# An encoder layer with gathered and dense experts: v sums of one gathered tile moved behind the dense weights, and weight loads of 1 MB

## The chip, the cores and the metric

One NeuronCore of a Trainium2 chip runs the whole program in one launch. The metric is device time in microseconds (us); three timed runs of the kernel before gave 3608.81, 3620.37 and 3621.52, a median of 3620.37.

## What is computed

One layer of a streaming encoder, in float32, over two request groups that share one set of weights: a prompt of 1024 rows and a sample of 64 rows, 1024 columns each. The layer projects the normed rows (`w_in`, 9224 columns), mixes three branches (an mLSTM memory, a spatial gating unit, cross-attention into 256 memory rows), projects back (`w_out`), and adds PEER, an expert layer:

```python
q = (xb @ w_pq)                                  # 8 heads, two half keys each
v1, i1 = lax.top_k(s1, 16); v2, i2 = lax.top_k(s2, 16)
sc, pos = lax.top_k(cand, 16)                    # cand: all 16 x 16 sums of v1 and v2
e = cidx at pos; g = softmax(sc)                 # 128 experts of 16384 for each row
a = gelu(einsum('tkd,td->tk', u_exp[e], xb))
out = einsum('tk,tkd->td', g * a, v_exp[e])
```

A final RMSNorm follows. `u_exp` and `v_exp` have 16384 rows of 1024 floats, 64 MB each.

## The kernel before

The 1088 rows are nine tiles: 0 to 7 of the prompt (128 rows each) and "s" (64 rows). **Phase 1** runs them in three blocks, [0, 1], [2, 3, 4, "s"] and [5, 6, 7], through all projections. Every float32 product is three passes on TensorE: the weights are split in a high and a low part (`w_split`, L267: ScalarE makes `wh` at L277, VectorE subtracts for `wl` at L280) and each piece of 128 rows by 512 columns, here called a *split*, is one `wh` and one `wl`. Pieces come from DRAM by `w_load` (L253) on SP's queue: 512 KB each, two splits, three buffers `wraw` and in phase 2 a fourth, `wrawx`. A new load is issued when a piece's last split is made.

The expert layer is done in two ways. Tiles 2, 3, 4 and 5 are **dense**: all 16384 experts go through TensorE in **phase 2** (`hidden` L1108 for u, L1268 to L1270 for v), each hidden value multiplied by its weight. These weights (mostly zeros) are made before that by the loop at L1189 to L1222: VectorE makes one-hot rows (L1197, L1201), TensorE multiplies them (L1210), and they go to DRAM (`gd`) and come back (`g`, L1098). When the last are made, the signal "weights" is given.

Tiles 0, 1, "s", 6 and 7 (`GT`) are **gathered** (`experts`, L939). Each of 128 columns (64 for "s") of such a tile needs two operations: *u* gathers 128 rows of `u_exp` by an indirect DMA that GpSimd issues (L1025, 512 KB) and takes their dot products on VectorE (L1038); *v* gathers rows of `v_exp` and adds them, each times its weight `w`, into `gacc` (L1046; for the last tile into `gx`). A u and a v buffer set of 3 and 4 (`gu`, `gv`) bounds what is under way. There are 576 u and 576 v operations; their list `ops` (L989) pairs the u of one tile with the v of the tile before. The weights `w` of a tile (`w2`, L959) need all its u; the `ops` wait for "weights" at the last u of "s" (L1066 to L1068), and tiles 6 and 7 are chosen only after it (L847).

What stands where on each engine is fixed when the program is built: `Flow` (L29) runs the generators by the costs that they yield (2.5 or 2.2 for each gathered operation, L1071), and a scheduler orders what they record. On the chip each engine then works through its list in order, and waits at each semaphore.

The v sum that is moved, and the retrieval whose chosen experts it shares VectorE with (`top16`, L797), stand in this code:

Of the kernel before, what the change touches and what calls it, by code (L numbers as in the profile page):

```python
# [7 lines left out]
F32 = mybir.dt.float32  # L8
# [6 lines left out]
ALU = mybir.AluOpType  # L15
# [3 lines left out]
D = 1024  # L19
# [6 lines left out]
O_Q, O_K, O_V, O_IG, O_FG, O_OG, O_SU, O_SV, O_XQ, O_GT = 0, 512, 1024, 2048, 2052, 2056, 3080, 4104, 5128, 6152  # L26
# [39 lines left out]
def tile_stream_step(ctx: ExitStack, tc: tile.TileContext, a: dict, out: dict):  # L66
    nc = tc.nc
    V, S, T, G, SP = nc.vector, nc.scalar, nc.tensor, nc.gpsimd, nc.sync
# [21 lines left out]
    mp = first.enter_context(tc.tile_pool(name="mp", bufs=1))  # L90

    BU, BV = 3, 4
    RAW, HL = 3, 4

    now = {"dp": None}

# [47 lines left out]
        return t  # L144

    wg_raw = mp.tile([128, KD, 8], F32, name="wg_raw", tag="sA")
    G.dma_start(wg_raw, a["w_in"][:, O_IG:O_IG + 8].rearrange("(k p) c -> p k c", p=128))

    wgh = mp.tile([128, 2, KD, 4], F32R, name="wgh")
    wgl = mp.tile([128, 2, KD, 4], F32R, name="wgl")  # L150
# [91 lines left out]
    pieces = []  # L242

    def want(src, c0):
        for kp in range(4):
            pieces.append(src[kp * 256:(kp + 1) * 256, c0:c0 + 512].rearrange("(k p) c -> p k c", p=128))


    POOL = 192, 224
    W = {"load": 0, "split": 0, "got": 0}  # L250
    raw_t, split_t = {}, {}

    def w_load():  # L253
        i = W["load"]
        if i >= len(pieces):
            return
        src = pieces[i]

        if now["dp"] is None or i % (RAW + 1):
            t = wp.tile([128, D], F32, name="wraw", bufs=RAW)  # L260
        else:
            t = now["dp"].tile([128, D], F32, name="wrawx")
        SP.dma_start(t.rearrange("p (k c) -> p k c", k=src.shape[1]), src)
        raw_t[i] = t
        W["load"] += 1

    def w_split():  # L267
        i = W["split"]
        if i >= 2 * len(pieces):
            return  # L270
        p, kk = divmod(i, 2)
        while W["load"] <= p:
            w_load()
        t = raw_t[p][:, kk * 512:(kk + 1) * 512]
        h = wp.tile([128, 512], F32R, name="wh", bufs=HL)
        l = wp.tile([128, 512], F32R, name="wl", bufs=HL)
        S.copy(h, t)  # L277

        E = G if POOL[0] <= i < POOL[1] else V
        E.tensor_tensor(l, t, h.bitcast(F32), op=ALU.subtract)  # L280
        split_t[i] = (h, l)
        W["split"] += 1
        if kk == 1:
            raw_t.pop(p)
            w_load()

    def w_get():
        i = W["got"]
        while W["split"] <= min(i + HL - 1, 2 * len(pieces) - 1):
# [45 lines left out]
    st = {}  # L335
# [233 lines left out]
    def want_block():  # L569
        for c in (O_K, O_Q, O_V, O_V + 512, O_SV, O_SV + 512, O_SU, O_SU + 512, O_GT + D, O_GT + D + 512,  # L570
                  O_XQ, O_XQ + 512, O_OG, O_OG + 512, O_GT, O_GT + 512, O_GT + 2 * D, O_GT + 2 * D + 512):
            want(a["w_in"], c)
        for c in (0, 512):
            want(a["w_out"], c)
        for c in (0, 512, 1024, 1536):
            want(a["w_pq"], c)

    def main():
        mem = memory()
# [10 lines left out]

    for nm in ("w_mk", "w_mv"):
        for c in (0, 512):
            want(a[nm], c)
    for _ in BLOCKS:
        want_block()

# [3 lines left out]
    GP = 4  # L600
    LG = 4

    def want_u(m):
        if m < NP:
            for r in range(2):
                pieces.append(a["u_exp_t"][r * 512:(r + 1) * 512, m * 256:(m + 1) * 256]
                              .rearrange("(k p) e -> p k e", p=128))

    for m in range(LG):
        want_u(m)  # L610
    for g in range(NP // GP):
        for j in range(2 * GP):
            if j % 2 == 0:
                want_u(GP * g + j // 2 + LG)
            hf, q = divmod(j, GP)
            e0 = (GP * g + q) * 256
            pieces.append(a["v_exp"][e0:e0 + 256, hf * 512:(hf + 1) * 512].rearrange("(k p) c -> p k c", p=128))


    def mlstm():  # L620
# [174 lines left out]
    NC = 54  # L795

    def top16(v, i, src, n):  # L797
        w = kp.tile([128, 128], F32, name="tk", bufs=4)[0:src.shape[0]]
        V.max(v[:, 0:8], src)
        V.max_index(i[:, 0:8], v[:, 0:8], src)  # L800
        V.match_replace(w[:, 0:n], v[:, 0:8], src, NEG)
        V.max(v[:, 8:16], w[:, 0:n])
        V.max_index(i[:, 8:16], v[:, 8:16], w[:, 0:n])
# [36 lines left out]
    def choose_tile(b, t):  # L840

        L = ROWS_OF[t]
# [6 lines left out]
        pos = kp.tile([128, 8, 16], U32, name="pos", bufs=1)[0:L]  # L849
# [14 lines left out]
        q = kp.tile([128, 6, 128], BF, name="pq_")[0:L]  # L864
# [34 lines left out]
        if t not in DENSE:  # L899
# [3 lines left out]
            e = gp.tile([128, 128], I32, name="e", bufs=3)  # L903

            for q in range(128 // L):
                V.scalar_tensor_tensor(e[q * L:q * L + L, 0:L], ef[:, q * 64:q * 64 + L], 128.0,
                                       ef[:, 128 + q * 64:128 + q * 64 + L], op0=ALU.mult, op1=ALU.add)
        gg = kp.tile([128, 8, 16], F32, name="ggd")[0:L]
        V.tensor_tensor(gg, scv, scv[:, :, 0:1].to_broadcast([L, 8, 16]), op=ALU.subtract)
        S.activation(gg, gg, AF.Exp)  # L910
        sm = kp.tile([128, 8], F32, name="ksm")[0:L]
# [18 lines left out]
    GT = [t for t in TILES if t not in DENSE]  # L930
# [8 lines left out]
    def experts():  # L939

        st_u, st_v, st_x = {}, {}, {}
# [12 lines left out]
        def end_u(t):  # L954
            _, av = st_u.pop(t)
            e, gg = st.pop(("e", t))
            L = ROWS_OF[t]
            av, gg = av[:, 0:L], gg[:, 0:L]
            t1 = gp.tile([128, 128], F32, name="w2", bufs=2)[:, 0:L]  # L959
            if t == GT[2]:  # L960
                V.tensor_copy(t1[0:1, 0:1], st["weights"][0:1])
            S.activation(t1, av, AF.Square, scale=GELU_C ** 0.5)
            V.scalar_tensor_tensor(t1, t1, 1.0, av, op0=ALU.add, op1=ALU.mult)
            S.activation(t1, t1, AF.Tanh, scale=GELU_S)
            V.scalar_tensor_tensor(t1, t1, 1.0, av, op0=ALU.add, op1=ALU.mult)
# [24 lines left out]
        for k in range(len(GT) + 1):  # L990
            u = [("u", GT[k], j) for j in range(ROWS_OF[GT[k]])] if k < len(GT) else []
            v = [("v", GT[k - 1], j) for j in range(ROWS_OF[GT[k - 1]])] if k > 0 else []
            m = max(len(u), len(v))
            for j in range(m):
                for l in (u, v):
                    lo, hi = j * len(l) // m, (j + 1) * len(l) // m
                    ops += l[lo:hi]
        inflight = []
        gt_, pvs = {}, {}
        nxt = 0  # L1000
        cnt = {"u": 0, "v": 0}
# [28 lines left out]
        def consume(op):  # L1030
            kind, t, j = op
            if kind == "u":
                tl = gt_.pop(op)
                if j == 0:
                    load_xn(t)
                _, av = st_u[t]
                xn = st_x[t]
                V.scalar_tensor_tensor(tl, tl, 1.0, xn, op0=ALU.mult, op1=ALU.mult, accum_out=av[:, j:j + 1])  # L1038
                cnt["u"] -= 1
                if j == ROWS_OF[t] - 1:  # L1040
                    end_u(t)
                return
            if j == 0:
                pvs[t] = begin_v(t)
            x2 = pvs[t]
            V.scalar_tensor_tensor(x2, gt_.pop(op), st_v[t][1][:, j:j + 1], x2, op0=ALU.mult, op1=ALU.add)  # L1046
            cnt["v"] -= 1
            if j == ROWS_OF[t] - 1:
                finish(t, pvs.pop(t))
# [254 lines left out]
def _layout(i):  # L1304
# [31 lines left out]
    d["w_mk"] = c(g["w_mk"][0])
    d["w_mv"] = c(g["w_mv"][0])
    d["w_out"] = c(g["w_out"][0])
    d["w_pq"] = c(g["w_pq"][0])
# [33 lines left out]
```

## Time and profile before

| what | value |
|---|---|
| median of 3 runs | 3620.37 us |
| profiled execution | 3614.62 us, span 3612.6 us |
| TensorE busy / VectorE busy | 3267.4 us (90%) / 3102.9 us (86%) |
| GpSimd busy / ScalarE busy | 1669.1 us (46%) / 1369.6 us (38%) |
| moved by DMA | 1024.77 MB, 284 GB/s over the span |
| GpSimd's queue (gathers) | 604.58 MB, 47.5% of 16 DMA engines |
| SP's queue (weights and the rest) | 413.06 MB, 34.2% of 16 DMA engines |

Time outside the span is 2.0 us. The busy shares are means over stages with different limits, so the table says little of a change in one stage; the rows by stage further down do. A stage that shows VectorE near its length and TensorE well under it, with a granted clock under 1, is one in which TensorE waits.

### The profile page before, as it was taken

To read this page: it belongs to the slowest core of one execution; us is meant where nothing else is said; L and a number is where in the kernel's file an instruction comes from. 1 tells how busy PE (TensorE), PEld (TensorE's weight loads), DVE (VectorE), ACT (ScalarE), POOL (GpSimd) and SP (SyncE) were. 2 spreads that over 40 slices of the span, in tenths; PEclk is the share of its full clock that TensorE was granted. 3 is DMA by queue.
4 is the path that set the end of the run, shared out by engine and by line. 5 is a ranking of instruction groups with operands and counts; after the bars stand their busy time and mean duration, and the time that the engine had idled before them with its cause. 6 is when DMAs were issued, how large, how long until landed. Compare 5 with 4: busy or idle time off the path is not lost.

```text
span 3612.6 us, 46174 instructions
## 1 busy us (share of the span) xinstructions
PE 3267.4 (90%) x15364; PEld 2633.3 (73%) x15364; DVE 3102.9 (86%) x6493; ACT 1369.6 (38%) x2481; POOL 1669.1 (46%) x1208
## 2 busy tenths in 40 slices
PE   8999999689998488699958896999999999999998
PEld 7787876467667366576756895888778888887886
DVE  5555798868999999989998998998789888887998
ACT  5555534223333234333324673333223333332332
POOL 1000448866656672654431004565456455544654
PEclk9999999799999789799978897999999999999999
DMA  7455578889898787898876558999889999988997
GB/s 236 146 164 178 176 260 310 290 264 354 315 360 307 271 279 234 287 320 280 289 243 197 169 172 283 342 353 331 298 307 382 334 341 336 344 309 297 385 345 261
DMA packets 447436, 1024.77 MB, mean 284 GB/s; under 512 B 32183, under 2 KB 169567, under 8 KB 443101
## 3 DMA queue, kind: packets, MB, share of 16 engines
q0 software_dynamic: 166528, 604.58, 47.5%
q1 hardware_dynamic: 276828, 413.06, 34.2%
q10 hardware_dynamic: 3840, 4.20, 0.3%
q8 instruction: 120, 1.97, 0.2%
q14 instruction: 120, 0.98, 0.1%
HBM read 968.44 MB, written 53.26 MB: 283 GB/s over the span
## 4 chain that ended last, share of the span: by engine, by line
PE 66%; DVE 13%; issue 9%; DMA 7%; POOL 4%; ACT 1%; SPq 0%; DVEq 0%; POOLq 0%; ACTq 0%
PE acc L311 6%; PE acc L312 6%; PE acc L313 6%; PE ph L1121 5%; PE ph L1119 5%; PE ph L1120 5%; PE po L1270 5%; PE po L1268 5%; PE po L1269 5%; PE po L1210 4%; DMA gu<-in_u_exp_dram,e 4%; POOL gu L1025 3%; PE acc L330 3%; PE acc L328 3%; PE acc L329 3%
## 5 line engine op out<-in xcount | busy, mean ns | idle before, releaser
L277 ACT CAST wh<-wraw 128x512 fp32r<-128x512 f32 x994 | 612.8, 621 | 1352.4 <-PE ph L1120 459.7
L1025 POOL DMA_INDIRECT gv<-in_v_exp_dram,e x522 | 720.1, 1380 | 864.0 <-DVE gacc L1046 307.9
L1025 POOL DMA_INDIRECT gu<-in_u_exp_dram,e x506 | 698.6, 1381 | 606.3 <-DVE gu L1038 404.9
L280 DVE TENSOR_TENSOR wl<-wraw,wh 128x512 fp32r<-128x512 f32 x962 | 654.3, 686 | 231.5 <-ACT wh L277 228.9
L1038 DVE SCALAR_TENSOR_TENSOR gu<-gu,gx 128x1024 f32<-128x1024 f32 x506 | 613.7, 1217 | 105.5 <-DMA gu<-in_u_exp_dram,e 103.9
L1046 DVE SCALAR_TENSOR_TENSOR gacc<-gv,w,gacc 128x1024 f32<-128x1024 f32 x448 | 572.3, 1278 | 6.1 <-DMA gv<-in_v_exp_dram,e 5.7
L312 PE MATMUL acc<-wl,half 128*128 128x512 f32 (+1 forms) x1152 | 475.1, 413 | 12.0 <-DVE wl L280 10.4
L313 PE MATMUL acc<-wh,half 128*128 128x512 f32 (+1 forms) x1152 | 457.2, 403 | 0.0
L311 PE MATMUL acc<-wh,half 128*128 128x512 f32 (+1 forms) x1152 | 414.0, 411 | 18.5 <-ACT uB L470 15.7
L1268 PE MATMUL po<-wh,W 128*128 128x512 f32 x1024 | 399.4, 398 | 31.2 <-ACT W L1238 30.6
L1269 PE MATMUL po<-wl,W 128*128 128x512 f32 x1024 | 407.9, 398 | 4.5 <-DVE wl L280 4.5
L1121 PE MATMUL ph<-dxh,wl 128*128 128x512 f32 x1024 | 401.7, 392 | 7.2 <-DVE wl L280 7.1
L1270 PE MATMUL po<-wh,W 128*128 128x512 f32 x1024 | 407.2, 398 | 0.6 <-DVE W L1239 0.6
L1119 PE MATMUL ph<-dxh,wh 128*128 128x512 f32 x1024 | 400.3, 391 | 1.3 <-DVE dxl L1143 1.3
L1120 PE MATMUL ph<-dxl,wh 128*128 128x512 f32 x1024 | 399.8, 390 | 0.0
L311 PEld LDWEIGHTS acc<-wh,half 128*128 128x128 f32 (+1 forms) x1152 | 210.8, 184 | 89.3 <-ACT uB L470 16.9
L312 PEld LDWEIGHTS acc<-wl,half 128*128 128x128 f32 (+1 forms) x1152 | 212.6, 185 | 80.9 <-DVE wl L280 16.6
L328 PE MATMUL acc<-half,wh 128*128 128x256 f32 (+2 forms) x768 | 250.4, 345 | 16.9 <-ACT wh L277 13.4
L329 PE MATMUL acc<-half,wh 128*128 128x256 f32 (+2 forms) x768 | 258.6, 342 | 0.0
L313 PEld LDWEIGHTS acc<-wh,half 128*128 128x128 f32 (+1 forms) x1152 | 211.6, 185 | 54.8 <-issue 1.7
L1268 PEld LDWEIGHTS po<-wh,W 128*128 128x128 f32 x1024 | 193.8, 189 | 78.8 <-issue 32.3
L330 PE MATMUL acc<-half,wl 128*128 128x256 f32 (+2 forms) x768 | 226.8, 342 | 18.4 <-DVE wl L280 18.4
(450 smaller groups left out, 5271.1 us busy)
## 6 DMA issues: line engine op xcount, KB each, us to landing
wraw<-in_w_in_dram SPq DMA_DIRECT2D x216, 512.0 KB
wraw<-in_v_exp_dram SPq DMA_DIRECT2D x126, 512.0 KB
wraw<-in_u_exp_t_dram SPq DMA_DIRECT2D x67, 512.0 KB
gd<-sg SPq DMA_DIRECT2D x16, 2048.0 KB
g<-gd SPq DMA_DIRECT2D x32, 1024.0 KB
wrawx<-in_u_exp_t_dram SPq DMA_DIRECT2D x61, 512.0 KB
wraw<-in_w_pq_dram SPq DMA_DIRECT2D x48, 512.0 KB
wraw<-in_w_out_dram SPq DMA_DIRECT2D x24, 512.0 KB
```

What stands on the lines that cost most here:

```text
L277: S.copy(h, t)
L280: E.tensor_tensor(l, t, h.bitcast(F32), op=ALU.subtract)
L311: T.matmul(ps[i], xh[:, cs], h, start=(k == 0), stop=False)
L312: T.matmul(ps[i], xh[:, cs], l, start=False, stop=False)
L313: T.matmul(ps[i], xl[:, cs], h, start=False, stop=(last and b is None))
L1025: G.indirect_dma_start(out=tl, out_offset=None, in_=src, in_offset=bass.IndirectOffsetOnAxis(ap=col, axis=0))
L1038: V.scalar_tensor_tensor(tl, tl, 1.0, xn, op0=ALU.mult, op1=ALU.mult, accum_out=av[:, j:j + 1])
L1119: T.matmul(o, h[:, cs], xh[:, k + kk, :], start=(k + kk == 0), stop=False)
L1121: T.matmul(o, l[:, cs], xh[:, k + kk, :], start=False, stop=(k + kk == KD - 1))
L1268: T.matmul(o, hi, h, start=(q == 0 and k == 0), stop=False)
L1269: T.matmul(o, hi, l, start=False, stop=False)
L1270: T.matmul(o, lo, h, start=False, stop=(q == GP - 1 and k == 1))
```

## The change

Two things are changed, and some small buffers have fewer copies or share their place.

The v operations of tile 1 are cut in two. The first 64 stay beside the u of "s"; the other 64 are put at the head of the next round, beside the u of tile 6, hence behind "weights". Their 64 columns of `w` are copied into a tile of their own (`w3`) at that point, and `w2` has one buffer where it had two.

The host lays the weights out anew, so that a piece is 1 MB with 8192 contiguous bytes for each partition: four splits for two. The runs were 2048 bytes (`w_in`, `w_out`, `w_pq`, `w_mk`, `w_mv`, `v_exp`) and 1024 bytes (`u_exp_t`). There are two buffers of 1 MB, in both phases, for three (four) of 512 KB. The first 56 pieces (the memory's and block 0's) come in two DMAs of 512 KB with runs of 4096 bytes. The eight gate columns, runs of 32 bytes before, have their own array.

```diff
-    RAW, HL = 3, 4
+    RAW, HL = 2, 4
+    W1 = 56
...
     def want(src, c0):
-        for kp in range(4):
-            pieces.append(src[kp * 256:(kp + 1) * 256, c0:c0 + 512].rearrange("(k p) c -> p k c", p=128))
+        for kp in range(2):
+            pieces.append(src[c0 // 512, kp])
...
-        if now["dp"] is None or i % (RAW + 1):
-            t = wp.tile([128, D], F32, name="wraw", bufs=RAW)
-        else:
-            t = now["dp"].tile([128, D], F32, name="wrawx")
-        SP.dma_start(t.rearrange("p (k c) -> p k c", k=src.shape[1]), src)
+        t = wp.tile([128, 2 * D], F32, name="wraw", bufs=RAW)
+
+        n = D if i < W1 else 2 * D
+        for c in range(0, 2 * D, n):
+            SP.dma_start(t[:, c:c + n], pieces[i][:, c:c + n])
...
-        p, kk = divmod(i, 2)
+        p, kk = divmod(i, 4)
...
-        if kk == 1:
+        if kk == 3:
             raw_t.pop(p)
             w_load()
...
             v = [("v", GT[k - 1], j) for j in range(ROWS_OF[GT[k - 1]])] if k > 0 else []
+            if k == 2:
+                v, late = v[:64], v[64:]
+            elif k == 3:
+                v = late + v
...
-            V.scalar_tensor_tensor(x2, gt_.pop(op), st_v[t][1][:, j:j + 1], x2, op0=ALU.mult, op1=ALU.add)
+            w = late_w[0][:, j - 64:j - 63] if t == GT[1] and j >= 64 else st_v[t][1][:, j:j + 1]
+            V.scalar_tensor_tensor(x2, gt_.pop(op), w, x2, op0=ALU.mult, op1=ALU.add)
...
                 yield "weights"
+                w = gp.tile([128, 64], F32, name="w3")
+                V.tensor_copy(w[0:1, 0:1], st["weights"][0:1])
+                V.tensor_copy(w, st_v[GT[1]][1][:, 64:128])
+                late_w.append(w)
...
-        w = kp.tile([128, 128], F32, name="tk", bufs=4)[0:src.shape[0]]
+        w = kp.tile([128, 128], F32, name="tk", bufs=2)[0:src.shape[0]]
...
-        gg = kp.tile([128, 8, 16], F32, name="ggd")[0:L]
+        gg = kp.tile([128, 8, 16], F32, name="ggd", tag="pos", bufs=1)[0:L]
...
-            t1 = gp.tile([128, 128], F32, name="w2", bufs=2)[:, 0:L]
+            t1 = gp.tile([128, 128], F32, name="w2", bufs=1)[:, 0:L]
...
+    def parts(m):
+
+        return c(m.reshape(2, 4, 128, -1, 512).transpose(3, 0, 2, 1, 4).reshape(-1, 2, 128, 2048))
...
+    d["u_exp_p"] = c(g["u_exp"][0].reshape(64, 256, 8, 128).transpose(0, 3, 2, 1).reshape(64, 128, 2048))
+    d["v_exp_p"] = c(g["v_exp"][0].reshape(32, 2, 2, 128, 2, 512).transpose(0, 4, 3, 1, 2, 5).reshape(32, 2, 128, 2048))
```

The built programs show where this puts VectorE's work. The first place is late in block 2, at the last retrieval (`top16`) before the dense weights. `MAX`, `MAX_INDEX` and `MATCH_REPLACE` are the retrieval's, and L1046 the v sums of tile 1. Before:

```order
L1046 SCALAR_TENSOR_TENSOR gacc<-gv,w_17933,gacc 128x1024
L801 MATCH_REPLACE tk<-v_14879,sc 128x128 x4
L1046 SCALAR_TENSOR_TENSOR gacc<-gv,w_17933,gacc 128x1024
L802 MAX v_14879<-tk 128x8 x4
L799 MAX v_14879<-sc 128x8 x4
L1046 SCALAR_TENSOR_TENSOR gacc<-gv,w_17933,gacc 128x1024
L803 MAX_INDEX i_14880<-v_14879,tk 128x8 x4
L800 MAX_INDEX i_14880<-v_14879,sc 128x8 x4
L1046 SCALAR_TENSOR_TENSOR gacc<-gv,w_17933,gacc 128x1024
```

And in the changed program, at the same place (the 580th `wl` of VectorE stands just ahead in both):

```order
L795 MAX v_14641<-sc 128x8 x2
L797 MATCH_REPLACE tk<-v_14801,sc 128x128
L795 MAX v_14641<-sc 128x8 x2
L798 MAX v_14801<-tk 128x8
L796 MAX_INDEX i_14642<-v_14641,sc 128x8
L795 MAX v_14712<-sc 128x8 x2
L796 MAX_INDEX i_14642<-v_14641,sc 128x8
L795 MAX v_14712<-sc 128x8 x2
L798 MAX v_14801<-tk 128x8
L796 MAX_INDEX i_14642<-v_14641,sc 128x8 x2
```

The v sums between the retrieval's rows are gone. Counted over VectorE's whole list, 567 gathered operations stand ahead of the first one-hot row (L1197) before and 512 now, and the last of the 512 stands far ahead of it, by the 512th `wl`. Ahead of that, the 16 `wl` from the 384th on have 60 gathered operations beside them before and 91 now, and those from the 448th on 49 and 60.

The second place is the end of VectorE's list, from the last `wl` (the last split of phase 2) on. `ob` takes up the dense result and needs TensorE's last product; `gx` is the last gathered tile's sum. Before:

```order
L280 TENSOR_TENSOR wl<-wraw,wh 128x512
L1046 SCALAR_TENSOR_TENSOR gx<-gv,w_29893,gx 128x1024
L280 TENSOR_TENSOR wl<-wraw,wh 128x512
L1046 SCALAR_TENSOR_TENSOR gx<-gu,w_29893,gx 128x1024 x3
L1046 SCALAR_TENSOR_TENSOR gx<-gv,w_29893,gx 128x1024 x2
L1279 TENSOR_TENSOR ob<-ob,po 128x2x512
L190 TENSOR_SCALAR rs<-ssn 128x1
L1279 TENSOR_TENSOR ob<-ob,po 128x2x512
```

And now, from the last `wl` on:

```order
L279 TENSOR_TENSOR wl<-wraw,wh 128x512
L1047 SCALAR_TENSOR_TENSOR gx<-gu,w_29392,gx 128x1024 x3
L1047 SCALAR_TENSOR_TENSOR gx<-gv,w_29392,gx 128x1024 x3
L1283 TENSOR_TENSOR ob<-ob,po 128x2x512
L1047 SCALAR_TENSOR_TENSOR gx<-gv,w_29392,gx 128x1024
L1283 TENSOR_TENSOR ob<-ob,po 128x2x512
L1047 SCALAR_TENSOR_TENSOR gx<-gu,w_29392,gx 128x1024 x2
L1292 TENSOR_TENSOR dss<-dss 128x4
L1047 SCALAR_TENSOR_TENSOR gx<-gu,w_29392,gx 128x1024
L191 TENSOR_SCALAR rs<-dss 128x4
L1047 SCALAR_TENSOR_TENSOR gx<-gv,w_29392,gx 128x1024
```

Before, 5 v sums stand behind the last `wl`; now 75 do (10 of them in the rows above), and then the last tile's norm. SP's list has 560 loads of weights before, 512 KB each; now 112 of 512 KB and 224 of 1 MB.

## Rows read from the trace of the kernel before

**Rows 1.** Stages: length, busy PE, PEld, DVE, ACT, POOL (xcount), granted clock, DMA share, GB/s

```profile
1163.00:1293.00 130.00, 66.36 (x318) 58.37 (x318) 126.28 (x410) 30.34 (x53) 89.67 (x60) 0.69 0.82 278
1293.00:1423.00 130.00, 129.10 (x563) 98.64 (x562) 121.49 (x452) 62.50 (x130) 56.11 (x35) 0.99 0.75 251
1423.00:1527.00 104.00, 61.98 (x230) 44.24 (x229) 96.50 (x219) 29.10 (x61) 64.93 (x50) 0.75 0.85 287
1527.00:1690.00 163.00, 155.39 (x691) 125.02 (x690) 148.69 (x331) 60.05 (x111) 86.72 (x58) 0.97 0.89 303
1690.00:1768.00 78.00, 61.21 (x253) 46.60 (x252) 75.91 (x195) 24.48 (x53) 36.28 (x28) 0.87 0.82 269
1768.00:1842.00 74.00, 74.00 (x445) 72.82 (x444) 72.05 (x182) 33.88 (x61) 25.42 (x19) 1.00 0.90 310
1842.00:1930.00 88.00, 32.32 (x138) 26.32 (x137) 88.00 (x361) 15.44 (x30) 28.29 (x29) 0.59 0.69 215
1930.00:2182.00 252.00, 233.90 (x1758) 218.21 (x1756) 225.50 (x478) 174.77 (x359) 13.27 (x9) 0.93 0.58 174
2213.00:3587.00 1374.00, 1361.46 (x5858) 1102.51 (x5859) 1218.83 (x1662) 426.73 (x629) 735.04 (x564) 1.00 0.93 333
3587.00:3613.00 26.00, 10.06 (x43) 7.74 (x42) 18.40 (x40) 3.71 (x10) 0.00 (x0) 0.77 0.36 142
```

**Rows 2.** Chain that ended last, from 1842 us: start, length (us), what

```profile
1859.60 1.18 DVE gacc L1046
1862.88 1.18 DVE gacc L1046
...
2017.98 1.21 DVE gacc L935
2019.20 5.98 DMA out_yp_dram<-gacc
2025.44 0.92 DVE gacc L975
```

**Rows 3.** VectorE's timeline at the end: start, us, instruction [idle before <-releaser]

```profile
3586.52 0.69 DVE L280 TENSOR_TENSOR wl<-wraw,wh 128x512 fp32r<-128x512 f32 x1
3587.12 3.92 DVE L1046 SCALAR_TENSOR_TENSOR gx<-gu,w,gx 128x1024 f32<-128x1024 f32 x3
3591.08 2.61 DVE L1046 SCALAR_TENSOR_TENSOR gx<-gv,w,gx 128x1024 f32<-128x1024 f32 x2
...
3596.84 0.15 DVE L190 TENSOR_SCALAR rs<-ssn 128x1 f32<-128x1 f32 x1
...
3600.82 1.28 DVE L935 SCALAR_TENSOR_TENSOR gx<-gx,rs,gfin 128x1024 f32<-128x1024 f32 x1
...
3603.60 4.87 DVE L935 SCALAR_TENSOR_TENSOR ob<-ob,rs,gfin 128x1024 f32<-128x1024 f32 x4
```

**Rows 4.** GpSimd's timeline near the end, the first of three like it, same columns

```profile
3561.24 1.49 POOL L1025 DMA_INDIRECT gu<-in_v_exp_dram,e  x1 [0.30 <-issue]
```

**Rows 5.** GpSimd's issues of gathers alone in 100 us: length, busy (xcount), clock, DMA, GB/s

```profile
3319.00:3419.00 100.00, 66.86 (x49) 1.00 0.98 369
```

**Rows 6.** A stretch of phase 2 with u operations almost alone, columns of Rows 1

```profile
2500.00:2700.00 200.00, 191.97 (x815) 152.87 (x814) 156.54 (x244) 58.10 (x87) 87.54 (x73) 0.99 0.87 300
```

**Rows 7.** DMA issues, 2872 to 2882 us: tile, queue, xcount, KB or us to landing

```profile
g<-gd SPq DMA_DIRECT2D x1, 1024.0 KB
gv<-in_v_exp_dram,e POOLq DMA_INDIRECT x3, 9.2
```

**Rows 8.** The same view, 2885 to 2915 us

```profile
gv<-in_v_exp_dram,e POOLq DMA_INDIRECT x8, 6.5
gu<-in_u_exp_dram,e POOLq DMA_INDIRECT x5, 6.0
```

**Rows 9.** DMA queues of the page: packets, MB, share of 16 engines

```profile
q0 software_dynamic: 166528, 604.58, 47.5%
q1 hardware_dynamic: 276828, 413.06, 34.2%
```

More of the change, by code (lines that the diff above doesn't have):

```diff
@@ L146, in tile_stream_step @@
     wg_raw = mp.tile([128, KD, 8], F32, name="wg_raw", tag="sA")
-    G.dma_start(wg_raw, a["w_in"][:, O_IG:O_IG + 8].rearrange("(k p) c -> p k c", p=128))
+    G.dma_start(wg_raw, a["w_gate"])
     wgh = mp.tile([128, 2, KD, 4], F32R, name="wgh")
@@ L256, in w_load @@
             return
-        src = pieces[i]
-        if now["dp"] is None or i % (RAW + 1):
-            t = wp.tile([128, D], F32, name="wraw", bufs=RAW)
-        else:
-            t = now["dp"].tile([128, D], F32, name="wrawx")
-        SP.dma_start(t.rearrange("p (k c) -> p k c", k=src.shape[1]), src)
+        t = wp.tile([128, 2 * D], F32, name="wraw", bufs=RAW)
+        n = D if i < W1 else 2 * D
+        for c in range(0, 2 * D, n):
+            SP.dma_start(t[:, c:c + n], pieces[i][:, c:c + n])
         raw_t[i] = t
@@ L268, in w_split @@
         i = W["split"]
-        if i >= 2 * len(pieces):
+        if i >= 4 * len(pieces):
             return
-        p, kk = divmod(i, 2)
+        p, kk = divmod(i, 4)
         while W["load"] <= p:
@@ L288, in w_get @@
         i = W["got"]
-        while W["split"] <= min(i + HL - 1, 2 * len(pieces) - 1):
+        while W["split"] <= min(i + HL - 1, 4 * len(pieces) - 1):
             w_split()
@@ L571, in want_block @@
                   O_XQ, O_XQ + 512, O_OG, O_OG + 512, O_GT, O_GT + 512, O_GT + 2 * D, O_GT + 2 * D + 512):
-            want(a["w_in"], c)
+            want(a["w_in_p"], c - (8 if c > O_FG else 0))
         for c in (0, 512):
-            want(a["w_out"], c)
+            want(a["w_out_p"], c)
         for c in (0, 512, 1024, 1536):
-            want(a["w_pq"], c)
+            want(a["w_pq_p"], c)
     def main():
@@ L592, in tile_stream_step @@
         for c in (0, 512):
-            want(a[nm], c)
+            want(a[nm + "_p"], c)
     for _ in BLOCKS:
@@ L604, in want_u @@
         if m < NP:
-            for r in range(2):
-                pieces.append(a["u_exp_t"][r * 512:(r + 1) * 512, m * 256:(m + 1) * 256]
-                              .rearrange("(k p) e -> p k e", p=128))
+            pieces.append(a["u_exp_p"][m])
     for m in range(LG):
@@ L611, in tile_stream_step @@
     for g in range(NP // GP):
-        for j in range(2 * GP):
-            if j % 2 == 0:
-                want_u(GP * g + j // 2 + LG)
+        for j in range(0, 2 * GP, 2):
+            want_u(GP * g + j // 2 + LG)
             hf, q = divmod(j, GP)
-            e0 = (GP * g + q) * 256
-            pieces.append(a["v_exp"][e0:e0 + 256, hf * 512:(hf + 1) * 512].rearrange("(k p) c -> p k c", p=128))
+            pieces.append(a["v_exp_p"][(GP * g + q) // 2, hf])
     def mlstm():
@@ L997, in experts @@
                     ops += l[lo:hi]
-        inflight = []
+        late_w = []
         gt_, pvs = {}, {}
@@ L1088, in two_banks @@
         return ps_d.tile([128, 2, 512], F32, name="po", bufs=2)
-    w_load()
     g4s = {}
@@ L1321, in _layout @@
     d["g_mem_t"] = c(g["g_mem"][0].reshape(8, 128).T)
-    d["w_in"] = c(g["w_in"][0])
+    w = g["w_in"][0]
+    d["w_gate"] = c(w[:, O_IG:O_IG + 8].reshape(8, 128, 8).transpose(1, 0, 2))
+    def parts(m):
+        return c(m.reshape(2, 4, 128, -1, 512).transpose(3, 0, 2, 1, 4).reshape(-1, 2, 128, 2048))
+    d["w_in_p"] = parts(np.concatenate([w[:, 0:O_IG], w[:, O_OG:]], axis=1))
     d["b_in"] = c(b)
@@ L1335, in _layout @@
     d["b_s_t"] = c(bs)
[L1336 to L1339, printed above, removed]
+    d["w_mk_p"] = parts(g["w_mk"][0])
+    d["w_mv_p"] = parts(g["w_mv"][0])
+    d["w_out_p"] = parts(g["w_out"][0])
+    d["w_pq_p"] = parts(g["w_pq"][0])
     d["k_sub_t"] = c(np.stack([g["k_sub1"][0].T, g["k_sub2"][0].T], axis=1))
@@ L1342, in _layout @@
     d["v_exp"] = c(g["v_exp"][0])
-    d["u_exp_t"] = c(g["u_exp"][0].T)
+    d["u_exp_p"] = c(g["u_exp"][0].reshape(64, 256, 8, 128).transpose(0, 3, 2, 1).reshape(64, 128, 2048))
+    d["v_exp_p"] = c(g["v_exp"][0].reshape(32, 2, 2, 128, 2, 512).transpose(0, 4, 3, 1, 2, 5).reshape(32, 2, 128, 2048))
     return d
```

## The prediction

> **What bounds the kernel now.** I read the stages first, because the busy shares of the whole span hide them. Phase 2 (2213 to 3587 us) has TensorE busy 1361.46 of 1374 us at a granted clock of 1.00 [rows 1]: TensorE is its limit, and nothing that makes VectorE or a transfer faster gives more than the 12.5 us between the two numbers. Behind it stand 26 us in which TensorE works 10 more [rows 1]. Ahead of it there are four stages in which VectorE is full and TensorE waits at a low clock: 1163 to 1293 us (VectorE 126.28 of 130, TensorE 66.36, clock 0.69), 1423 to 1527, 1690 to 1768 and 1842 to 1930 us (VectorE 88.00 of 88, TensorE 32.32, clock 0.59) [rows 1]. Between these lie stages that TensorE fills: 129.10 of 130, 155.39 of 163, 74.00 of 74 [rows 1]. The chain of waits says the same: from 1842 us it runs through v sums `gacc`, a start every 3.3 us with the retrieval's rows between, 1.18 us each [rows 2].
>
> So the gathered operations cost time in two ways before the weights: where VectorE is full, 1.2 us for each v sum; where TensorE is full, nothing. In phase 2 they cost nothing as long as they fit beside TensorE.
>
> **The change part by part.** *The 64 sums held.* GpSimd issues 60, 50, 28 and 29 gathers in the four VectorE-bound stages [rows 1]; VectorE's list has, at the same `wl`, 60, 49, 27 and 35 before (the last stretch reaches to 1979 us) and 91, 60, 0 and 0 now. The scheduler thus brings sums forward into the first two and clears the last two: +31 +11 −27 −35 = −20 sums, at 1.2 us −24 us. The other 44 leave stages that TensorE fills; of those only 1527 to 1690 us has room, 7.6 us of idle TensorE, and I take −8. While the weights are made (1930 to 2182 us) TensorE is busy 233.90 of 252 [rows 1], and a hole there belongs to tile 1: its norm at 2017.98, its output's store of 5.98 us, and the `gacc` that VectorE can only clear once that store has landed, at 2025.44 [rows 2]. All three move behind the weights: −10, from 2016 to 2026 us. Sum: −42 us up to the weights. Bounds: −87 if all 64 sums were on the path (77 + 10), −10 if only the hole goes.
>
> *Phase 2 with 64 more.* Their pace is fixed by the list: 18 to 20 gathered operations beside 16 splits, before as now. Phase 2 therefore does not grow; what doesn't fit stands behind its last `wl`, 75 sums for 5. That tail is the largest term. Before, 26.1 us lie between the start of the last `wl` (3586.52) and the end of the span (3612.6) [rows 3]. Now: TensorE ends 10 to 11 us after that `wl` [rows 1], and in the new list's end 6 sums stand ahead of the `ob` that waits for it; 11 us. Seven gathers have landed by then, one to each buffer, 7 at 1.2 = 8 us. The 62 left come at the pace of gather and sum. From below that is VectorE's 1.28 to 1.31 us (3.92 for three) [rows 3]; from above 2.04 us, 49 in 100 us at the best sustained stretch with TensorE's weights loading beside them [rows 5]. GpSimd alone, unhindered, starts one every 1.8 us (1.49 and 0.30 of idling) while VectorE is full [rows 4]. VectorE makes no splits in the tail, so I take the middle of the two ends, 1.66, just under GpSimd's: 103 us. Then the last tile's norm and store: from `rs` at 3596.84 to the end of its product 5.3 us, 1.3 us of squares ahead of that by my estimate from the product's length, and 4.1 us from VectorE's last row (3608.47) to the end [rows 3]: 11 us. In all 11 + 8 + 103 + 11 = 133 us for 26: +107. Bounds: 62 at 1.28 give +83, at 2.04 +130.
>
> *Loads of 1 MB.* Bytes are the same. The queue of 4096-byte rows takes 0.0786% of the engines' span per MB (47.5 for 604.58 MB), SP's, with its short runs, 0.0828% (34.2 for 413.06) [rows 9]; 5% cheaper loads would give SP's queue back 1.8 points of 34.2. In phase 2 TensorE's idle 12.5 us bound any gain. A loss is possible: beside a `g` load, the one load of 1 MB with 8192-byte runs that the kernel already has, a gather lands after 9.2 us, between two of them after 6.0 to 6.5 [rows 7, 8]. With seven buffers at 2.3 us an operation a gather may take 16 us, so that is hidden. Where u operations run alone, on three buffers, it is not: there TensorE was busy 191.97 of 200 us [rows 6]. Such stretches hold 95 u in phase 2 before (67 and 28), 50 now. Fewer and slower; I take 0 for phase 2, from −12 (the idle time) to +45 (50 at 0.9 us, a third of the 2.7 us by which a landing is later), nearest to zero because rows 6 lose only 8 us in 200. In phase 1 the DMA share is 0.58 to 0.90 in the stages shown [rows 1], so transfers seldom set the pace: 0, from −39 (1.8% of its 2182 us, were they the limit everywhere) to +15 (below).
>
> *The rest.* The copy into `w3` and the gates' array are one short row each beside full stages: nothing. `tk` with two copies changes the order of retrieval rows, not their number, all on one engine: nothing. `ggd` on the buffer of `pos` makes the next tile's `MAX_INDEX` wait for the store that SP makes of `ggd`; behind it on VectorE stand the splits that TensorE needs. Four tiles, a store of some 4 us each (the 4.1 us of the last one): +15 at worst, nothing where SP is not behind. `w2` with one copy makes the norm-like end of a tile's u wait for the last v of the tile before; the list has that order already, as the u-only stretches counted above.
>
> **Sum.** 3614.6 − 42 + 0 + 0 + 107 = 3679.6, so 3680 us. The profiled execution lies 5.8 us under the median of the three runs (3620.37) and within them; I leave that as it is.
>
> **The rivals.** *A: the gathers get slower as well.* Loads with 8192-byte runs come every 11 us instead of a `g` load every 44, so most gathers land as the one of rows 7 does. For it: 9.2 against 6.5 us. Against it: seven buffers hide 16 us. It decides if u-only stretches or the tail's end stall: +45, 3725 us. The Trainium skill, "DMA: Bandwidth & Descriptors", section "Queues, rings and completion order", says that each DMA engine takes turns between queues a packet at a time; longer packets of weights would by that take a larger share beside the gathers. Rows 7 and 8 agree with it; by it the sum would be rival A's.
>
> *B: faster.* VectorE's relief counts in full wherever the sums stood, because the four VectorE-bound stages are chained by buffers to the TensorE-bound ones: −87; phase 2 and the loads give their −12 and −39; and the tail, with DMA and GpSimd free, runs at VectorE's pace, +83. That is 3614.6 − 87 − 51 + 83 = 3560 us. For it: VectorE is 94% busy from 1163 to 2182 us (the eight stages summed). Against it: most of the sums that go had TensorE at 155.39 of 163 and 74.00 of 74 beside them [rows 1], and 42 come back into stages that are full. It decides only if all three terms lie at their ends together.
>
> *C: no change.* The 64 sums weigh the same in both places: −77 −10 ahead, +87 behind at 1.35 us a sum. 3614.6 us. For it: VectorE is the engine of both. Against it: GpSimd's 1.8 us.
>
> *D: the list is not kept to.* If 64 sums slipped in beside phase 2's splits, there would be no tail and the time would be 3614.6 − 42 = 3573. Against it: each engine follows its list, and the list puts them last.
>
> **How the numbers follow.** My forecast 0.66, with its own range 3645 to 3715; A 0.14; C 0.12; B 0.06; D 0.02. The range that should hold 8 in 10: the bounds of the terms give 3560 below and 3614.6 − 10 + 45 + 15 + 130 = 3795 above, all at their ends together; 3610 to 3735 takes in the forecast, A and about half of C, and leaves out some 0.15. A measurement of this kernel can tell about 0.5% (18 us) from no change: faster is under 3602, slower over 3638. Faster: B and D, 0.08. Same: C and the lowest edge of the forecast, 0.13. Slower: the rest of the forecast and A, 0.79.
>
> **What would show it.** Right: in the changed profile phase 2 still at a clock of 1.00 and near 1370 us; TensorE idle for its last 100 to 130 us, with 60 or more `gx` sums in that stretch, 1.5 to 1.9 us apart; the first one-hot row some 30 us earlier, and the stages before 1930 us where the retrieval stands alone shorter by the sums' 1.2 us each; the hole at 2016 gone. Wrong: a tail under 90 us, the one-hot rows earlier by 70 us or more, or phase 2 shorter by more than its idle 12 us. Rival A would show in landings of 8 us or more between 1 MB loads, and in TensorE's idle time where u run alone.

## The result and the profile after

The changed kernel takes 3678.67 us (median of 4 runs, 3675.56 to 3682.25) against 3618.47 for the kernel before beside it: a ratio of 1.0165, with a 95% interval of 1.0147 to 1.0184. Its profiled execution is 3679.57 us with a span of 3677.8.

The span is 65 us longer than before. Cut at the first dense product (first `po`) and at the last `wl`, it goes like this:

| stretch | before | after | difference | forecast |
|---|---|---|---|---|
| to the first `po` | 2210.6 | 2197.5 | −13 | −42 |
| first `po` to last `wl` | 1375.9 | 1363.7 | −12 | 0 |
| last `wl` to the end | 26.1 | 116.5 | +90 | +107 |

The sum is nearly the forecast's, but none of its three terms is. Here are the stages of the changed kernel, with the columns of [rows 1]. The first four are cut at the same `wl` as there. After that the cuts differ: 1764 to 1919 us here (four rows, 155 us) answers to 1690 to 1930 us there (three rows, 240 us).

```profile
1162.00:1343.00 181.00, 65.00 (x329) 56.80 (x328) 164.34 (x469) 32.26 (x57) 120.40 (x88) 0.66 0.83 283
1343.00:1467.00 124.00, 124.00 (x537) 92.32 (x536) 115.17 (x350) 57.70 (x108) 56.70 (x36) 1.00 0.78 265
1467.00:1596.00 129.00, 69.24 (x265) 48.80 (x264) 119.68 (x300) 35.78 (x84) 82.27 (x64) 0.74 0.85 295
1596.00:1764.00 168.00, 164.15 (x739) 131.72 (x738) 146.61 (x460) 66.23 (x131) 34.17 (x30) 0.99 0.65 212
1764.00:1843.00 79.00, 78.71 (x412) 68.64 (x411) 48.24 (x114) 37.12 (x67) 0.00 (x0) 1.00 0.49 173
1843.00:1883.00 40.00, 40.00 (x248) 40.00 (x247) 39.66 (x220) 17.51 (x30) 0.00 (x0) 1.00 0.37 125
1883.00:1919.00 36.00, 24.22 (x117) 19.96 (x117) 36.00 (x192) 14.94 (x32) 1.61 (x1) 0.72 0.30 107
1919.00:2168.00 249.00, 234.72 (x1762) 217.60 (x1761) 211.51 (x419) 170.35 (x349) 0.94 (x1) 0.96 0.51 151
2198.00:3561.00 1363.00, 1357.89 (x5859) 1103.65 (x5859) 1215.77 (x1677) 427.54 (x633) 747.97 (x559) 1.00 0.91 335
3561.00:3678.00 117.00, 10.81 (x47) 8.35 (x45) 107.79 (x111) 4.04 (x11) 73.88 (x70) 0.56 0.91 347
```

Read each row by its length and by TensorE's share. The first stage had 130 us for 66 us of TensorE's work and now has 181 for 65: GpSimd issues 88 gathers in it, not 60. The third went from 104 to 129 us. The later ones gained: the stage of the last retrieval, 88 us long in [rows 1], is 36 us, and no gather at all is issued from 1764 to 1883 us. Phase 2 has lost more than half of its idle time (TensorE is busy 1357.89 of 1363 us). The last row is the new tail: 117 us in which TensorE works 11.

In the first stage TensorE waits for the retrieval. The kernel after (engine, line, waited for: us in total, times, longest), in that stage:

```profile
ACT sc L818 <- DVE tk L797: 91.0, 8, 21.5
PEld ms L815 <- ACT sc L818: 84.9, 6, 23.4
```

and the kernel before, in the same stage (1163 to 1293 us):

```profile
ACT sc L822 <- DVE tk L801: 47.4, 6, 13.3
PEld ms L819 <- ACT sc L822: 34.8, 3, 13.3
```

A score's buffer comes free when VectorE has done its `MATCH_REPLACE` into `tk`; ScalarE's copy waits for that, and TensorE for the copy. A gathered operation that stands between the retrieval's rows on VectorE makes this chain longer: ScalarE's wait on it grew by 43.6 us where the stage grew by 51.

The tail, on VectorE (start, length, what; idle before it in brackets), answers to [rows 3]:

```profile
3561.27 0.69 DVE L279 TENSOR_TENSOR wl<-wraw,wh 128x512 fp32r<-128x512 f32 x1
3561.87 3.92 DVE L1047 SCALAR_TENSOR_TENSOR gx<-gu,w,gx 128x1024 f32<-128x1024 f32 x3
...
3570.44 1.22 DVE L1283 TENSOR_TENSOR ob<-ob,po 128x1024 f32<-128x1024 f32 x1 [0.69 <-PE po L1274]
...
3593.61 4.87 DVE L931 SCALAR_TENSOR_TENSOR ob<-ob,rs,gfin 128x1024 f32<-128x1024 f32 x4
...
3666.40 2.61 DVE L1047 SCALAR_TENSOR_TENSOR gx<-gv,w,gx 128x1024 f32<-128x1024 f32 x2
...
3672.53 1.29 DVE L931 SCALAR_TENSOR_TENSOR gx<-gx,rs,gfin 128x1024 f32<-128x1024 f32 x1
```

and on GpSimd, answering to [rows 4]:

```profile
3588.20 1.02 POOL L1025 DMA_INDIRECT gu<-in_v_exp_dram,e  x1 [0.30 <-issue]
...
3594.81 0.94 POOL L1025 DMA_INDIRECT gu<-in_v_exp_dram,e  x1 [0.30 <-issue]
3599.94 1.86 POOL L1025 DMA_INDIRECT gu<-in_v_exp_dram,e  x1 [4.19 <-DVE gx L1047]
```

Here an issue takes 1.02 and 0.30 us, together 1.32, just the pace of VectorE's sums (3.92 for three). Both engines run full, but for short waits around the `ob` rows. The longest is where four of these rows (4.87 us) hold VectorE: no buffer comes free, and GpSimd waits 4.19 us. 75 sums stand in this tail, as the list had it.

### The profile page after: what moved, and what is told of

It is laid out like the page before. It is cut to its first block, busy times and chain, and to the rows that moved or that the text cites. A ratio compares the mean times of both kernels' runs of the same rounds, so it can differ in the third digit from the quotient of the medians.

```text
span 3677.8 us, 45485 instructions
## 1 busy us (share of the span) xinstructions
PE 3247.4 (88%) x15364; PEld 2619.2 (71%) x15364; DVE 3113.5 (85%) x6495; ACT 1372.8 (37%) x2483; POOL 1622.4 (44%) x1208
## 3 DMA queue, kind: packets, MB, share of 16 engines
q1 hardware_dynamic: 140124, 413.05, 31.4%
## 4 chain that ended last, share of the span: by engine, by line
PE 50%; DVE 7%; issue 5%; DMA 4%; POOL 2%; ACT 0%; POOLq 0%; DVEq 0%; ACTq 0%; SPq 0%
PE ph L1125 6%; PE ph L1123 6%; PE ph L1124 6%; PE po L1272 6%; PE po L1274 6%; PE po L1273 6%; PE po L1214 5%; DMA gu<-in_u_exp_dram,e 3%; PE acc L311 2%; PE acc L310 2%; PE acc L312 2%; DVE gx L1047 2%; POOL gu L1025 1%; DVE gu L1038 1%; DVE gacc L1047 1%
## 5 line engine op out<-in xcount | busy, mean ns | idle before, releaser
L276 ACT CAST wh<-wraw 128x512 fp32r<-128x512 f32 x1120 | 690.0, 621 | 1436.0 <-PE ph L1124 465.6
L279 DVE TENSOR_TENSOR wl<-wraw,wh 128x512 fp32r<-128x512 f32 x1088 | 738.3, 685 | 275.2 <-ACT wh L276 272.7
L1025 POOL DMA_INDIRECT gu<-in_u_exp_dram,e x506 | 667.2, 1319 | 613.9 <-DVE gu L1038 379.1
L312 PE MATMUL acc<-wh,half 128*128 128x512 f32 (+1 forms) x1152 | 457.1, 402 | 0.0
L310 PE MATMUL acc<-wh,half 128*128 128x512 f32 (+1 forms) x1152 | 430.8, 412 | 18.9 <-ACT uB L469 17.3
```

Source lines behind the costliest of these rows:

```text
L310: T.matmul(ps[i], xh[:, cs], h, start=(k == 0), stop=False)
L312: T.matmul(ps[i], xl[:, cs], h, start=False, stop=(last and b is None))
L1025: G.indirect_dma_start(out=tl, out_offset=None, in_=src, in_offset=bass.IndirectOffsetOnAxis(ap=col, axis=0))
```

## The experiments

Eleven kernels tell three things apart: the hold of 64 sums, the longer loads, and the small buffers that the change makes smaller. Each was timed beside the kernel before; "first `po`", "phase 2" and "tail" are the table's three stretches in its profiled execution.

**The hold alone** (`hold_only`): the kernel before with `late`, `w3` and one `w2` as in the change; loads and `tk` as before.

```diff
+            if k == 2:
+                v, late = v[:64], v[64:]
+            elif k == 3:
+                v = late + v
```

> The kernel before with the 64 v sums held, and the weight loads as they were (512 KB). The list has 72 sums behind the last wl, and ahead of the weights no sums brought forward: 60 and 49 gathered operations beside the 16 wl from the 384th and 448th, as before. Theory 1 (two terms of opposite sign: a tail of 1.32 us a sum, and relief of VectorE only where the sums stood in full stages): tail 72 x 1.32 = 95 and 20 for the end less 26 = +87; relief 42 (last retrieval) + 11 + 12 (the hole) = -65; about 3635 us, the first dense product some 65 us earlier than 2213. Theory 2 (the hold alone makes the whole 60 us, the loads are innocent): about 3675 us, the first dense product near 2198.

Measured 3632.11 us, 1.0029 (1.0014 to 1.0044). Its first `po` is at 2156.2 us, 54 earlier than before, phase 2 is 1363.5 us and the tail 112.4, with 72 sums. Three of its stretches:

```profile
1845.00:1873.00 28.00, 16.04 (x90) 13.99 (x89) 28.00 (x163) 10.46 (x20) 1.61 (x1) 0.73 0.42 142
1873.00:2127.00 254.00, 240.74 (x1790) 223.00 (x1789) 218.71 (x455) 172.80 (x356) 0.13 (x1) 0.94 0.51 149
...
3520.00:3632.00 112.00, 10.19 (x44) 7.86 (x42) 103.32 (x107) 3.82 (x10) 69.98 (x67) 0.56 0.90 347
```

The relief all shows in one place: the last retrieval takes 28 us where [rows 1] have 88. And the built list now has 60 and 49 gathered operations beside the 384th and 448th `wl`, as before. So the hold does not bring sums forward; something else in the change does.

The 60 us are more than the sums of that stage. VectorE's v sums in the kernel before (count, busy us, mean ns), in that stage (1842 to 1930 us) and in the one ahead of it (1768 to 1842 us), which TensorE fills:

```profile
L1046 DVE SCALAR_TENSOR_TENSOR gacc<-gv,w,gacc 128x1024 f32<-128x1024 f32 x27 | 34.6, 1281 | 0.0
L1046 DVE SCALAR_TENSOR_TENSOR gacc<-gv,w,gacc 128x1024 f32<-128x1024 f32 x20 | 25.6, 1278 | 0.0
```

`hold_only` has none in either. The retrieval's `MATCH_REPLACE` rows in the stage that TensorE fills, before and then in `hold_only` (1772 to 1845 us):

```profile
L801 DVE MATCH_REPLACE8 tk<-v,sc 128x128 f32<-128x128 f32 x8 | 2.2, 279 | 0.0
L801 DVE MATCH_REPLACE8 tk<-v,sc 128x128 f32<-128x128 f32 x31 | 9.4, 307 | 0.0
```

So with the 20 sums gone, the retrieval gets done beside TensorE's work instead of behind it. The two stages took 162 us and take 101: the 61 us are about what all 47 sums took, 25.6 and 34.6.

**The rest without the hold** (`load_only`): the changed kernel with `late` and `w3` taken out.

> The changed kernel without the hold: loads of 1 MB and the small buffers alone. 9 sums behind the last wl; the list brings sums forward as in the changed kernel (91 and 62 beside the 16 wl from the 384th and 448th), all of tile 1 done by the 544th. Theory 1: no tail, about 3611 us (3600 to 3625), end 25 to 30 us behind the last wl. Theory 2 (long runs slow the gathers or starve the splits): 3640 us or more, with the loss spread over phase 2. Theory 3 (loads cost 5% less and phase 1 is paced by transfers): 3575 us or less.

Measured 3659.59 us, 1.0102 (1.0081 to 1.0124): a loss. No tail (29.1 us), but a first `po` at 2251.9 and a phase 2 of 1391.9 us (its profiled execution, 3674.66 us, is its longest). Its list has the sums brought forward, 91 and 62. Set beside the changed kernel, which has the same list but for the hold, it shows that the hold gives 54 us up to the first `po` here too (2197.5 for 2251.9), as it did in `hold_only` (2156.2 for 2210.6). The rest of the change loses 41 us there in both pairs (one trace for each kernel).

**Half of the hold** (`hold32`): the changed kernel with 32 sums held.

```diff
-                v, late = v[:64], v[64:]
+                v, late = v[:96], v[96:]
```

> The changed kernel with 32 sums held for 64. 46 sums behind the last wl for 75. Theory 1: the time is half way between no hold and 64 held in the tail's term, 29 x 1.32 = 38 us less than 75 have: about 3643 us less what 32 sums more ahead of the weights cost (0 to 38 us): 3640 to 3680. If the two cancel, the time stays at 3679: then a sum costs the same on either side. Theory 2 (the hold costs by its waits, whatever its number: w3, w2 with one copy): 3675 us with a tail shorter by 38.

Measured 3675.6 us, 1.0149 (1.0128 to 1.017), not to be told from the change. The tail is 38 us shorter (78.2 us for 46 sums, so 1.32 us a sum), the first `po` 24 us later (2221.2) and phase 2 12 longer. A sum costs about the same on either side of the weights.

**The held sums left out** (`drop63`): the changed kernel without 63 of the 64 held v operations, gathers too.

```diff
-                v, late = v[:64], v[64:]
+                v, late = v[:64], v[127:]
```

> The changed kernel with 63 of the 64 held sums (and their gathers) left out of the computation. The list up to the weights is that of the changed kernel; 10 sums stand behind the last wl for 75. Theory 1: the tail goes, 63 x 1.32 = 83 us: about 3596 us. Theory 2 (the held sums cost beside phase 2, by transfers, not behind it): phase 2 shorter than 1364 us by 20 or more and the time under 3580.

Measured 3613.82 us, 0.9975 (0.9964 to 0.9987), more than expected: the tail is gone (30.1 us), but the first `po`, at 2204.3, is only 6 us earlier than before, where `hold_only` gained 54. Even with the work gone, what the rest of the change loses ahead of it stays. And phase 2 is 1382.0 us, 18 more than with the held sums: without them beside the u of tile 6, TensorE idles 18 us in it, for 5.

**Two copies of `tk`** (`tk2_only`): the kernel before with that one number changed.

```diff
-        w = kp.tile([128, 128], F32, name="tk", bufs=4)[0:src.shape[0]]
+        w = kp.tile([128, 128], F32, name="tk", bufs=2)[0:src.shape[0]]
```

> The kernel before with one number changed: the retrieval's scratch tile tk has 2 copies for 4. The built list then brings gathered operations forward as the changed kernel's does: 92 beside the 16 wl from the 384th for 60, 61 from the 448th for 49. Theory 1 (that order is what costs: sums leave stages that TensorE fills, where they were free, for stages that VectorE fills, where each costs 1.2 us): 3655 us, the first dense product near 2250 us for 2211, the stage from the 384th wl longer by 40. Theory 2 (the loads of 1 MB cost what the load_only run lost): as before, 3620 us.

Measured 3641.48 us, 1.0058 (1.0039 to 1.0077), less than expected. The one number moves the sums: the built list has 92 and 61 at the two places. Its first stage, and TensorE's and ScalarE's waits in it:

```profile
1159.00:1343.00 184.00, 67.83 (x345) 59.22 (x345) 168.21 (x492) 34.40 (x62) 124.51 (x86) 0.65 0.84 285
```

```profile
PEld ms L819 <- ACT sc L822: 90.3, 6, 26.1
ACT sc L822 <- DVE tk L801: 77.0, 6, 22.3
```

The 184 us and the 86 gathers are nearly those of the change (181 and 88), with none of its other parts. At the 512th `wl` this kernel is 56 us behind the kernel before (1703.4 us for 1647.8), but its first `po` is only 16 us later (2226.8): the 47 sums that were brought forward are gone from the stretch behind the 544th `wl`, and that gives most of it back. Phase 2 is 12 us longer than before (1388.3); no run shows why.

**All small buffers** (`small_only`): `tk`, `w2` and `ggd` as in the change, nothing else.

```diff
-        gg = kp.tile([128, 8, 16], F32, name="ggd")[0:L]
+        gg = kp.tile([128, 8, 16], F32, name="ggd", tag="pos", bufs=1)[0:L]
```

> The kernel before with the changed kernel's three small buffers alone: tk 2 copies, ggd on the buffer of pos, w2 1 copy; loads of 512 KB with short runs, no hold. VectorE's list is that of load_only (92 and 63 gathered operations at the two places). Theory 1 (all that load_only lost comes from the list): 3658 us. Theory 2 (loads with longer runs cost by themselves what runs4k lost): 3641 us, the same as tk 2 alone.

Measured 3641.0 us, 1.0072 (1.0054 to 1.0091), theory 2's figure. `tk` alone and `ggd` alone (below) add up to 0.73%, so the single `w2` shows no cost of its own. `load_only` stands at 1.0102, so the 1 MB loads come to 0.30% or 11 us by themselves (18.6 between the two medians); the intervals of the two overlap, so this part is the least certain.

**`ggd` alone** (`ggd_only`): the edit just shown.

> The kernel before with ggd on the buffer of pos and nothing else. Its list is that of runs4k nearly row for row (7 to 9 gathered operations brought ahead of the 464th, 512th and 576th wl). Theory 1 (that list, and the wait of pos for the store of ggd, are what runs4k lost): 3640 us. Theory 2 (the runs are): 3620 us.

Measured 3622.57 us, 1.0015 (1.0001 to 1.0028); the list has 60 and 56, so this edit brings 7 sums forward at little cost.

**Runs of 4096 bytes** (`runs4k`): the new layout on the host, in pieces of 512 KB and three or four buffers as before; `tk` with four copies, `ggd` and `w2` as in the change, no hold.

```diff
-        for kp in range(4):
-            pieces.append(src[kp * 256:(kp + 1) * 256, c0:c0 + 512].rearrange("(k p) c -> p k c", p=128))
+        for kp in range(2):
+            for z in range(2):
+                pieces.append(src[c0 // 512, kp][:, z * D:z * D + D])
```

> The weights in the changed kernel's layout on the host, but loaded in pieces of 512 KB with 4096-byte runs into the buffers of before (3, then 4); tk with 4 copies; no hold. The list is that of before (60 and 49 gathered operations at the two places, 5 sums behind the last wl). Theory 1 (longer runs cost nothing and give little): 3605 to 3622 us. Theory 2 (longer runs slow the gathers): 3645 us, landings over 8 us in phase 2. Theory 3 (transfers pace phase 1): under 3590 us.

Measured 3641.3 us, 1.0057 (1.0041 to 1.0072), near theory 2's time. Its list has 60 and 56 at the two places, not 60 and 49; that is `ggd_only`'s. Against `ggd_only`, with the same small buffers but for `w2` and the same gathers at every place that I counted in VectorE's list, it is 0.42%, 15 us, with intervals apart. Longer runs and the new places of the pieces in DRAM come together here; no run separates them. The bytes went more cheaply through the DMA engines: the queue of the weights (packets, MB, share) in `runs4k`, where [rows 9] have 34.2%:

```profile
q1 hardware_dynamic: 172380, 413.06, 33.0%
```

But the gathers beside them landed later, by about half a microsecond. Issues from 2750 to 3200 us with the median us from issue to landing, before

```profile
gv<-in_v_exp_dram,e POOLq DMA_INDIRECT x108, 7.0
gu<-in_u_exp_dram,e POOLq DMA_INDIRECT x81, 7.1
```

and in `runs4k`

```profile
gv<-in_v_exp_dram,e POOLq DMA_INDIRECT x109, 7.5
gu<-in_u_exp_dram,e POOLq DMA_INDIRECT x82, 7.5
```

That is under theory 2's 8 us. VectorE's wait for gathered u rows (us in total, times, longest), in `ggd_only`

```profile
DVE gu L1038 <- DMA gu<-in_u_exp_dram,e: 90.2, 74, 5.1
```

in `runs4k`

```profile
DVE gu L1036 <- DMA gu<-in_u_exp_dram,e: 123.9, 68, 8.4
```

in `small_only`

```profile
DVE gu L1038 <- DMA gu<-in_u_exp_dram,e: 100.3, 72, 5.6
```

and in `load_only`

```profile
DVE gu L1034 <- DMA gu<-in_u_exp_dram,e: 152.9, 86, 11.0
```

Both pairs point the same way: longer runs, and VectorE waits 34 and 53 us more for u. The sizes are uncertain. Each is one trace against one; those of `ggd_only` and `small_only` are their kernels' shortest executions and those of `runs4k` and `load_only` their longest, and the same wait is 103.9 us in the kernel before and 112.1 in `tk2_only`, both with the short runs. The whole of phase 2, first in `ggd_only`, then in `runs4k`:

```profile
2209.00:3585.00 1376.00, 1360.36 (x5861) 1101.81 (x5862) 1220.85 (x1665) 428.84 (x631) 740.15 (x564) 1.00 0.93 333
```

```profile
2227.00:3622.00 1395.00, 1367.85 (x5860) 1105.52 (x5861) 1219.22 (x1664) 428.55 (x631) 743.19 (x564) 0.99 0.91 329
```

TensorE idles 27 us where it idled 16, and the DMA share falls: the DMA engines were less busy, yet the gathers came later.

**More copies of `tk`** (`tk5`): the kernel before with five.

> The kernel before with 5 copies of tk for 4. The list moves a little the other way: 7 gathered operations fewer ahead of the 400th, 512th and 576th wl. Theory 1: 7 sums leave full stages, 8 us: 3611 us. Theory 2 (4 copies were enough for the order to be free): 3619 us.

Measured 3602.42 us, 0.9957 (0.9941 to 0.9973): faster than both kernels. Its first stage:

```profile
1148.00:1272.00 124.00, 67.97 (x340) 59.03 (x339) 118.72 (x408) 35.50 (x60) 79.53 (x54) 0.75 0.79 266
```

**Five copies and 16 sums held** (`hold16_tk5`): `tk5` with the hold's edits (one `w2` among them) for the last 16 of the 64.

> The kernel before with 16 v sums held for none (as the change does it with 64) and 5 copies of tk. 29 sums behind the last wl for 5. Theory 1: tail +24 x 1.32 = +32; relief of the last retrieval and the weights -(16 + 7) x 1.2 = -28, the hole of tile 1's end -12, phase 2 -4: about 3608 us. Theory 2 (each sum held costs as much as it gives, and the hole moves along): 3620 us or more.

Measured 3613.08 us, 0.9981 (0.9972 to 0.999): above `tk5`, though the intervals touch. Its first `po` came 10 us earlier (2177.9 for 2188.4), its tail was 29 us longer (55.1 for 25.9, with 29 sums), and its phase 2 was 9 shorter.

**Six copies of `tk`, one `w2`** (`tk6_w21`).

> The kernel before with 6 copies of tk, and w2 with 1 copy to make room (alone that moves nothing in the list). 328 gathered operations ahead of the 400th wl for 350 before and 343 with 5 copies, 560 for 576 ahead of the 592nd. Theory 1 (the fewer sums in full stages the better): 3590 us, 10 less than with 5 copies. Theory 2 (with 5 copies nothing is left to gain, 16 sums more fall into the weights' making): 3602 us or more.

Measured 3625.7 us, 1.0017 (1.0007 to 1.0028), as theory 2 had it. Its list has 36 and 49 at the two places, `tk5`'s 50 and 51. More copies are not simply better: each number gives another list. What `tk5` owes its gain to, beyond the 6 us of its first stage and the earlier `po`, stays open.

## Why the prediction held in the sum and not in each step

In ratios to the kernel before, the parts put on one after the other give +0.72% (small buffers), +0.30% (loads), +0.63% (hold): 26, 11 and 23 us, 60 in all. In the other order the hold alone is +0.29%, 10 us. Whether the parts add up independently stays open: the intervals of the two figures for the hold overlap.

- **"`tk` with two copies changes the order of retrieval rows, not their number, all on one engine: nothing."** This step failed: alone it costs +0.58%. The number stayed, but the order decided in which stage the gathered sums stand. In `tk2_only` 47 sums left the stretch behind the 544th `wl`, where the last retrieval stands, for the first and the third stage, where the retrieval's chain runs through VectorE. It cost 56 us there and gave back 40.
- **The relief of 42 us up to the weights.** Measured: 13. I counted the sums that move right (+31, +11, −27, −35) but took the hold for their cause; `hold_only` has 60 and 49. As the counts were of the whole change, this did not alter the sum. The prices did. At the 512th `wl` the changed kernel is 66 us behind the kernel before (1714.0 us for 1647.8), where 42 sums at 1.2 us were to cost 50; 88 gathers take 181 us in the first stage, 2.06 us each. From there to the first one-hot row it gains 79 us, where I had 74. The −8 in a stage with room and the −10 of the hole did not come as such. In the stage with room TensorE's idle time went from 7.6 to 3.9 us. From the first one-hot row to the first `po` both kernels take 291 us, and in the 10 us of [rows 2] that I took for a hole, VectorE waited 1.2 us (before, 1930 to 2182 us):

```profile
DVE gacc L975 <- DMA out_yp_dram<-gacc: 1.2, 1, 1.2
```

- **"... where TensorE is full, nothing."** This failed too. In `hold_only` the last retrieval's stage shrank by 60 us, because the 20 sums in the stage ahead of it, with TensorE at 74.00 of 74, had pushed the retrieval's rows back. VectorE was full in both stages (72.05 of 74 and 88.00 of 88), and all 47 sums counted, at 1.28 us. That made −54, above my −42, without the hole and without the roomy stage.
- **Phase 2, 0 us.** Measured −12, the bound. TensorE's idle time in it went from 13 to 5 us, 8 of the 12. With the held sums beside the u of tile 6, fewer u run alone, and VectorE's wait for gathered u rows in phase 2 falls; before, then after:

```profile
DVE gu L1038 <- DMA gu<-in_u_exp_dram,e: 51.7, 43, 3.6
DVE gu L1038 <- DMA gu<-in_u_exp_dram,e: 23.4, 14, 4.8
```

- **The tail, +107.** Measured +90: the mechanism and the count (75 sums) were right, the pace was not: 1.32 us a sum in place of 1.66. The 1.8 us of [rows 4] were no bound on GpSimd, and a full VectorE is not what made them: in the last retrieval's stage of [rows 1], with VectorE at 88.00 of 88, 28 gathers were issued in 26.7 us, 0.95 us each, less than the tail's 1.02. What makes an issue longer elsewhere, no run here separates. The sum of 62 at 1.32 is 82, not 103, 21 less; the waits around the `ob` rows took some 4 of that back.
- **Loads of 1 MB, 0 us.** Measured some +11 (15 with the shorter runs), inside the bounds. Rival A's direction is right, since gathers land later beside longer runs, but its sign was not seen: landings were to come after 8 us or more, and `runs4k` has 7.5, the changed kernel 7.5 and 7.0. Its size was not +45, and in the changed kernel phase 2 shows none of it. The Trainium skill, "DMA: Bandwidth & Descriptors", section "Queues, rings and completion order", has the engines take turns between queues a packet at a time; the later landings beside `runs4k`'s longer runs (7.5 for 7.0 and 7.1 us) go the way of that, but no run here counted packets in turn.
- **Rival C, no change**, weighed the sums the same on both sides. That is nearly so (`hold32`), and the hold alone, at +10 us, is no change by the 0.5% of the prediction. **Rival D** fell: 75 sums stood last, as listed. **Rival B** had the tail (+83) and phase 2 (−12) nearly right, and that sums count beside a full TensorE too; it fell with its −87 up to the weights (−13) and its −39 for the loads (a loss).

So the forecast of 3680 for 3679 is luck as far as the number goes. Errors cancelled: 29 us of relief that did not come, against 17 of tail too much and the 12 of phase 2 that were not forecast. The direction and the largest term, the tail, were not luck.

## What to carry to other kernels

Where a scheduler orders recorded work, a scratch buffer's count is an input of the schedule: compare the built lists for each edit alone before an effect of the list is put down to the edit that one has in mind. Work put behind the last stage costs its own sustained pace there (1.32 us a sum), so it pays only if each unit costs more where it comes from. Here 64 sums gave 54 us ahead of the first `po` and 12 in phase 2 and cost 86 behind it (`hold_only`). A stage that one engine fills can still hide a cost on another: sums there pushed the next stage's work back. Loads that use the DMA engines better can still cost time, if gathers on another queue set the pace beside them.

## What was not expected of the hardware

- GpSimd issued an indirect gather of 512 KB every 1.32 us (1.02 and 0.30 idle) in the tail, where VectorE does little but sums, with 347 GB/s in that stretch; one came every 2.06 us in the first stage, where an issue took 1.37 us (120.40 for 88) and VectorE is busy with the retrieval as well.
- Runs of 4096 bytes for 1024 and 2048 lowered the weights' DMA share from 34.2 to 33.0%, of 8192 bytes to 31.4%. In both cases VectorE waited longer for gathered rows: 123.9 and 152.9 us, for 88 to 112 us in the kernels with the short runs and no hold.
